# Row tiles of 128 with two meta rows apart, weight blocks visited forward, backward and forward, a written order of the row steps, and a fifth feed-forward unit begun among the first four

## The chip, the cores and the metric

The kernel runs on one core of a Trainium2 chip. Its engines are TensorE (PE), VectorE (DVE), ScalarE (ACT) and GpSimd (POOL); SyncE (SP) issues most of the DMAs. Each engine takes its instructions in the order in which they are queued. The metric is the device time of one execution in microseconds, as the median of several runs.

## The reference, cut to what matters

The program is one decoder layer on 1024 rows of 1024 values. Two mixers (a gated linear recurrence and a pooling mixer) give `z`. The part in question is the product `z @ w_out`, the two norms around the residual, and the start of the gated feed-forward network:

```python
h = h + rmsnorm(z @ w_out[l], mix_norm_post[l])
u = rmsnorm(h, ffn_norm_pre[l])
gt = causal_dwconv(u @ ffn_w_gate[l], ffn_conv_w[l], ffn_conv_b[l])
y = (jax.nn.gelu(gt, approximate=True) * (u @ ffn_w_up[l])) @ ffn_w_down[l]
h = h + rmsnorm(y, ffn_norm_post[l])
return h[:, N_META:]
```

There are 16 meta rows ahead of the 1024. Behind the mixers only the last two are needed, since the convolution looks back over two rows: 1026 rows go through the mixer output and the feed-forward network.

## The kernel before, in words

**Numbers.** Every float32 operand is split into a high and a low part, and a product is three matmuls (`mm3`, L171 to L176): high by high, high by low, low by high. A stationary operand has up to 128 columns, a moving one 512.

**Mixer output.** `z` lies as eight blocks `k` of 128 x 1026, transposed. The output is worked in three chunks `c` of 342 rows, each of three row tiles of 114 (`CW`, `RT`). In a chunk the loop runs over the eight blocks of `w_out`; a block meets the three tiles, two halves of 512 columns and three parts, 18 matmuls. The results `pm` lie in PSUM, a pair of banks a tile, of four pairs. A block of `w_out` is a DMA of 512 KB (`wraw`), a cast to `whi` on ScalarE and, in the first chunk, a low part `wlo` on GpSimd that is also stored to `wlos`. The two later chunks load the raw block and the stored low part again: 24 raw loads and 16 low parts in all. SBUF holds three blocks at a time (`AHEAD`). `split_z` (L1097) makes the high and low part of `z`, one chunk and block at a time.

**Row steps.** A finished tile goes through these steps, which class `Rows` holds: `take` squares it on ScalarE with an accumulator and multiplies it by a gain on DVE; `add` makes the root, the reciprocal and, on DVE, the residual sum, and stores the rows to `hscr`; `norm` squares again and makes `un`; `feat` transposes `un` by eight PE transposes (`pt`) and makes the features in `to_quarters`. The feed-forward product takes the rows as two halves (Strassen's scheme), so the features go to the quarters `b11`, `b21` (first half) and `b12`, `b22` (second half) and to the sums `t1` to `t4`, each with a high part (ScalarE) and a low part (DVE or GpSimd). `by_rows` divides each store and load of a row tile into two DMAs, of 112 and 2 rows.

**Order.** In this part `manual_schedule` is on: PE, ScalarE, DVE and GpSimd run their instructions as the Python code writes them, one list for each engine. SyncE's DMAs are issued as the code reaches them, and wait in one queue. The row steps of a chunk stand between the blocks of the next one; in the last chunk the last three blocks are taken tile by tile.

**The feed-forward units.** `Strassen` plans 22 units of seven products P1 to P7. P1 and P2 need only the first half of the rows, so those of units 0 to 3 (`EARLY`) stand before the rest, with the features of the last three tiles between them; then come P3 to P7 of unit 0 (`rest`) and the other units (`finish`), of which unit 4 (`UP0`) starts with its P1. Weights of these first units are split early and kept in DRAM (`kept`, in the order `KEPT`). `whole` turns finished quarters of a unit into gates, with a convolution on DVE; `swa` and `swb` are sums of weights on GpSimd.

Of the kernel before, what the change touches and what calls it, by code (L numbers as in the profile page):

```python
# [23 lines left out]
CW = TQ // 3  # L24
HEADS = 4
# [34 lines left out]
def trunk_kernel(ctx: ExitStack, tc: tile.TileContext, x, meta_tokens, mix_norm_pre,  # L60
# [117 lines left out]
    def proj(w, col, n_k, xs, chunks, ws=None, name="pj"):  # L178
# [5 lines left out]
        for k in range(n_k):  # L184
            for (lo, n), ps in zip(chunks, banks):
                xhi, xlo = xs(k, lo, n)
                pe.matmul(ps[:, :n], whi[:, k, :], xhi, start=(k == 0), stop=False)
                pe.matmul(ps[:, :n], whi[:, k, :], xlo, start=False, stop=False)  # L188
            for (lo, n), ps in zip(chunks, banks):
                xhi, _ = xs(k, lo, n)  # L190
                pe.matmul(ps[:, :n], wlo[:, k, :], xhi, start=False, stop=(k == n_k - 1))
        return banks

    class Strassen:
# [8 lines left out]
        def __init__(self, units, run, early, quarters, halo, put, whole):  # L203
# [8 lines left out]
            self.got, self.at, self.kept = [], 0, []  # L212
# [118 lines left out]
        def rest(self, u, between=None):  # L331
# [13 lines left out]
            self.whole(u, 0)  # L345
            dve.tensor_tensor(own, own, self.product(u, "P7"), ALU.add)  # L346
            self.put(u, 1, 1, own, x5)
            self.put(u, 1, 0, u2, self.product(u, "P4"))
            self.whole(u, 1)

        def finish(self, at=0):
            for i in range(at, len(self.run)):
                u = self.run[i]
                if i + 1 < len(self.run):
                    self.load_unit(self.run[i + 1])
                if u >= self.early:
                    for f in self.first(u):
                        f()
                self.rest(u)
# [525 lines left out]
    KEPT = [(e + i, p) for e in range(0, EARLY, 2) for p in ("P1", "P2") for i in range(2)]  # L885
    KEPT += [(0, p) for p in Strassen.ORDER[2:]] + [(UP0, p) for p in Strassen.ORDER]
# [211 lines left out]
    def split_z(c, k):  # L1098
        zc = slot(2 * CW, F32R, "zc")
        zh, zl = zc[:, :CW], zc[:, CW:]  # L1100
        act.copy(zh, z[k][:, c * CW : (c + 1) * CW])
        dve.tensor_tensor(zl, z[k][:, c * CW : (c + 1) * CW], rr(zh), ALU.subtract)
# [4 lines left out]
    for kind, i in order:  # L1107
# [23 lines left out]
        banks = proj(None, 0, n_k, xs, chunks, ws=ws, name="p" + kind.lower())  # L1131
# [16 lines left out]
    fq = {}  # L1148
    for n, name, names in ((HT, "v1", ("b11h", "b11l", "b21h", "b21l")), (HN, "v2", ("b22h", "b22l", "t1h", "t1l"))):
        t = ubig(F32R, name).rearrange("p (i k t) -> p i k t", i=4, k=4)  # L1150
# [10 lines left out]
    RT = CW // 3  # L1161
# [4 lines left out]
    def wo_parts(c, k):  # L1166
        if c == 0:
            (hi, lo), = wsplit(wblock(w_out[0], k, 1, 0, D), 1, D, pool_e)
            pool_e.dma_start(wlos[k], rr(lo[:, 0]))
            return [(hi, lo)]  # L1170
# [3 lines left out]
        nc.sync.dma_start(rr(lo), wlos[k])  # L1174
        act.copy(hi, raw)
        return [[t.rearrange("p (k c) -> p k c", k=1) for t in (hi, lo)]]

    wo = Loader([(c, k) for c in range(3) for k in range(KD)], wo_parts)

    def by_rows(move):  # L1180

        for r in (slice(0, RT - HALO), slice(RT - HALO, RT)):
            move(r)

    def load_res(t0):
        row = slot(D, name="row2")
        if t0 == 0:
            nc.sync.dma_start(row[:HALO], meta_tokens[T0:NM, :])
            nc.sync.dma_start(row[HALO:RT], x[0, 0 : RT - HALO, :])
        else:  # L1190
            by_rows(lambda r: nc.sync.dma_start(row[r], x[0, t0 - HALO + r.start : t0 - HALO + r.stop, :]))
# [5 lines left out]
    def to_quarters(un, t_at, banks, eng):  # L1197

        for j in range(2):
            for i in range(4):  # L1200
                k = 4 * j + i
                pe.transpose(banks[j][:, i * RT : (i + 1) * RT], un[:RT, k * P : (k + 1) * P], ident[:RT, :RT])
        srcs = [b_[:, : 4 * RT].rearrange("p (k t) -> p k t", k=4) for b_ in banks]
        n1 = max(0, min(RT, HT - t_at))
        if n1:
            for src, q in zip(srcs, ("b11", "b21")):
                put(q, src[:, :, :n1], slice(t_at, t_at + n1), dve)
        f = max(0, HT - t_at)
        n2 = RT - f
        if n2 <= 0:  # L1210
            return []
        s_ = slice(t_at + f - HT, t_at + RT - HT)
        d = slice(s_.start + HALO, s_.stop + HALO)
        b12, b22 = (src[:, :, f:] for src in srcs)

        t1, t2 = halves_tmp(n2)
        c12, c22 = halves_tmp(n2)
        act.copy(c12, b12)
        act.copy(c22, b22)

        def first_sums():
            combine(dve, t1, c12, ALU.subtract, "b11", d)
            dve.tensor_tensor(t2, c22, t1, ALU.subtract)
            put("t2", t2, d, dve)

        def difference():
            dve.tensor_tensor(c12, c22, c12, ALU.subtract)
            put("t3", c12, s_, dve)

        return [first_sums, lambda: put("t1", t1, s_, dve), lambda: put("b22", c22, s_, eng), difference,  # L1230
                lambda: negdiff(eng, t2, t2, "b21", d), lambda: put("t4", t2, d, eng)]

# [11 lines left out]
    rows, z_at = {}, {}  # L1244

    def next_z(n):

        for i in range(len(z_at), min(len(z_at) + n, 3 * KD)):
            z_at[i] = split_z(i // KD, i % KD)

    def mix_tile(c, k, w, x_, i):
        (whi, wlo), (zh, zl) = w, z_at[c * KD + k]
        t = slice(i * RT, (i + 1) * RT)
        for j in range(2):
            n = slice(j * 512, (j + 1) * 512)
            mm3(x_[:RT, n], (zh[:, t], zl[:, t]), (whi[:, 0, n], wlo[:, 0, n]), k == 0, k == KD - 1)

    class Rows:


        def __init__(self, c, tiles_):
# [422 lines left out]
```

## Time and profile before

| | |
|---|---|
| median of 3 runs | 1365.37 us |
| lowest and highest | 1363.81 and 1366.29 us |
| the profiled execution | 1364.63 us |
| its span in the trace | 1362.9 us |
| mean granted TensorE clock | 0.994 |
| mixer output in the trace | about 595.8 to 707.5 us |

The profile shows one execution. Busy times are of that span; a matmul is pipelined, so its duration overlaps the next, and the distance between two starts is what it costs. A wait names the line of the waiting instruction and, behind the arrow, the engine and line that released it; `DMA` there is a transfer. Names are those of the program's tiles, without numbers.

### The profile page before, as it was taken

Reading aid. Unit: us, or ns where it says so; the run is one execution under the profiler, and the core shown is the slowest. Engines: PE = TensorE matmul, PEld = TensorE weight load, DVE = VectorE, ACT = ScalarE, POOL = GpSimd, SP = SyncE. Lnnn points to the kernel's source line nnn. Section 1 sums busy time; section 2 is a strip of 40 time slices with the busy share of each in tenths; the row PEclk is TensorE's granted clock in tenths of the full one; section 3 lists DMA queues with packets and bytes.
Section 4 is the critical chain, followed back from the end, with each engine's and each line's share of the span. In section 5 each row is a group of like instructions: output and inputs, shape, how many; then the busy total and the mean of one; then the engine's idle time right before and its main releaser. Section 6 shows DMA issues by size and latency. Waiting matters only on the chain. (4 is left out here: it accounts for less than half of the span.)

```text
span 1362.9 us, 20069 instructions
## 1 busy us (share of the span) xinstructions
PE 1338.6 (98%) x7737; PEld 1187.0 (87%) x7737; DVE 955.9 (70%) x1246; ACT 566.2 (42%) x946; POOL 434.1 (32%) x328
## 2 busy tenths in 40 slices
PE   8999999999999999999999999999999999999997
PEld 7799999999999999987779888888888887888786
DVE  6755644489775757766568889888978776744557
ACT  6543333465555474226655222222222223543343
POOL 2014421236343700051020556454557742000100
PEclk9999999998999999999999999999999999999999
DMA  7134333311110159979877877656677799965524
GB/s 266 48 117 140 124 112 106 101 47 47 34 49 19 34 173 306 323 246 301 286 260 245 233 206 201 196 176 164 156 166 170 179 236 269 380 205 191 183 95 154
DMA packets 141453, 236.66 MB, mean 174 GB/s; under 512 B 9254, under 2 KB 77450, under 8 KB 141358
## 3 DMA queue, kind: packets, MB, share of 16 engines
q1 hardware_dynamic: 129294, 211.00, 46.0%
q0 software_dynamic: 12064, 24.38, 10.5%
q8 instruction: 61, 1.00, 0.3%
q14 instruction: 34, 0.28, 0.1%
HBM read 171.85 MB, written 86.53 MB: 190 GB/s over the span
## 5 line engine op out<-in xcount | busy, mean ns | idle before, releaser
L287 PE MATMUL P<-v,whi 128*128 128x512 f32 (+2 forms) x408 | 141.9, 356 | 2.2 <-DVE p L346 1.3
L288 PE MATMUL P<-v,whi 128*128 128x512 f32 (+2 forms) x408 | 141.2, 353 | 0.0
L290 PE MATMUL P<-v,wlo 128*128 128x512 f32 (+2 forms) x424 | 136.0, 351 | 0.0
L175 PE MATMUL pd<-rot 128*128 128x512 f32 x272 | 105.9, 389 | 0.3 <-DVE rot L1417 0.3
L176 PE MATMUL pd<-rot 128*128 128x512 f32 x272 | 105.8, 389 | 0.0
L141 POOL TENSOR_TENSOR wlo<-wraw,whi 128x1024 fp32r<-128x1024 f32 (+1 forms) x19 | 44.7, 2353 | 169.7 <-ACT whi L140 99.1
L1417 DVE TENSOR_TENSOR rot<-yt,rot 128x1024 fp32r<-128x1024 f32 x33 | 41.2, 1249 | 70.1 <-ACT rot L1416 70.1
L287 PEld LDWEIGHTS P<-v,whi 128*128 128x128 f32 x408 | 77.2, 189 | 13.2 <-DVE p L346 1.7
L232 ACT CAST whi<-wraw 128x512 fp32r<-128x512 f32 x78 | 46.1, 618 | 98.1 <-PE P L288 79.1
L288 PEld LDWEIGHTS P<-v,whi 128*128 128x128 f32 x408 | 77.2, 189 | 10.7 <-issue 0.2
L290 PEld LDWEIGHTS P<-v,wlo 128*128 128x128 f32 x424 | 74.3, 189 | 11.4
L233 DVE TENSOR_TENSOR wlo<-wraw,whi 128x512 fp32r<-128x512 f32 x74 | 68.4, 946 | 20.1 <-ACT whi L232 20.1
L1305 POOL TENSOR_TENSOR ys<-y 128x512 f32<-128x512 f32 x22 | 35.6, 1617 | 137.5 <-DVE y L1363 52.6
L174 PE MATMUL pd<-rot 128*128 128x512 f32 x272 | 72.7, 390 | 2.0 <-ACT rot L1416 1.2
L258 POOL TENSOR_TENSOR swa<-wraw,wraw 128x512 f32<-128x512 f32 x28 | 44.4, 1586 | 92.6 <-DMA wraw<-in_w_in_dram 51.2
L140 ACT CAST whi<-wraw 128x1024 fp32r<-128x1024 f32 (+1 forms) x28 | 26.4, 943 | 109.0 <-PE ppv L188 21.7
L1416 ACT CAST rot<-yt 128x1024 fp32r<-128x1024 f32 x33 | 34.6, 1052 | 87.8 <-PE pd L175 87.8
L232 ACT CAST whi<-swa 128x512 fp32r<-128x512 f32 x56 | 33.4, 619 | 85.0 <-PE P L288 76.5
L1349 DVE SCALAR_TENSOR_TENSOR y<-g,par,y 128x1024 f32<-128x1024 f32 x44 | 63.9, 1451 | 0.8
L174 PEld LDWEIGHTS pd<-rot 128*128 128x128 f32 x272 | 50.9, 188 | 13.5 <-ACT rot L1416 1.8
L175 PEld LDWEIGHTS pd<-rot 128*128 128x128 f32 x272 | 51.0, 188 | 11.3 <-DVE rot L1417 0.7
L176 PEld LDWEIGHTS pd<-rot 128*128 128x128 f32 x272 | 51.1, 188 | 10.7
(389 smaller groups left out, 4172.2 us busy)
## 6 DMA issues: line engine op xcount, KB each, us to landing
wraw<-in_w_in_dram SPq DMA_DIRECT2D x36, 512.0 KB
yt<-ysum SPq DMA_DIRECT2D x33, 512.0 KB
wraw<-in_ffn_w_gate_dram SPq DMA_DIRECT2D x26, 512.0 KB
wraw<-in_w_out_dram SPq DMA_DIRECT2D x24, 512.0 KB
wraw<-in_ffn_w_up_dram SPq DMA_DIRECT2D x22, 512.0 KB
wsum<-in_ffn_w_down_dram SPq DMA_DIRECT2D x22, 512.0 KB
ysum<-ys SPq DMA_DIRECT2D x11, 768.0 KB
sa<-sscr SPq DMA_DIRECT2D x16, 513.0 KB
```

The costliest lines, as they stand in the source:

```text
L141: eng.tensor_tensor(lo, raw, rr(hi), ALU.subtract)
L174: pe.matmul(ps, ahi, bhi, start=first, stop=False)
L175: pe.matmul(ps, ahi, blo, start=False, stop=False)
L176: pe.matmul(ps, alo, bhi, start=False, stop=last)
L232: act.copy(hi, src)
L233: (pool_e if 4 <= i < 2 * self.early else dve).tensor_tensor(lo, src, rr(hi), ALU.subtract)
L258: pool_e.tensor_tensor(s1, a21, a22, ALU.add)
L287: pe.matmul(d, whi[:, k, :], xh[:, c : c + w], start=(k == 0 and onto is None), stop=False, **go)
L288: pe.matmul(d, whi[:, k, :], xl[:, c : c + w], start=False, stop=False, **go)
L290: pe.matmul(x[:, o : o + w], wlo[:, k, :], xh[:, c : c + w], start=False, stop=(k == 3), **go)
L1349: dve.scalar_tensor_tensor(a, g[:, j : j + SEQ], cvw[:, j, m : m + 1], a, ALU.mult, ALU.add)
L1417: dve.tensor_tensor(lo, src, rr(hi), ALU.subtract)
```

## The change

**Tiles.** The 1024 rows are eight tiles of 128, in chunks of two, three and three (`TILES`). The two meta rows are a tile of their own in the first chunk (`mix_meta`): high and low part of `z` stand side by side as four stationary columns, so that four matmuls a block do (four columns by `whi` and two by `wlo`, for each half). Low and high results then lie in different rows; `join` copies them out of PSUM, moves two rows by DMA (`pml`), and `joined` adds them.

**Weights.** The blocks are visited 0 to 7, 7 to 0 and 0 to 7 (`KS`). Class `Mixer` keeps the last three blocks over a turn: 18 raw loads and 10 low parts. Every chunk takes its last two blocks tile by tile (`LAST`).

**Row steps.** Class `Row` holds one tile, with `root`, `scale` and `square` as steps of their own. The tables `SEAM` and `SEAM4` write which step stands after which block, tile or product. `negdiff` is always on GpSimd, the low part of `b22` of tiles 4, 5 and 6 too, and that of `t4` for tile 4. Features of the first half are one cast and one subtraction of 1024 columns. Row tiles are stored and loaded by one DMA each.

**Units.** P1 and P2 of unit 4 stand among those of units 2 and 3 (`BEGUN`), and its multiplication by the gate waits for `finish` (`mul_up`). `rest` loads the weights two units ahead, before P4's sums, and unit 0's `whole` of the first half comes after its P7.

**Projection.** The last product before the mixer output (`pba`) does its last two blocks bank by bank (`by_bank`).

```diff
+TILES = ((0, 1), (2, 3, 4), (5, 6, 7))
+KS = (range(8), range(7, -1, -1), range(8))
+LAST = 2
+LATE_ON_POOL = tuple(HALO + i * P for i in (4, 5, 6))
+SEAM = (("W", "W", "W", "W", "W", "W", "0.take 0.add", "W 0.square 1.take m.join 0.norm 1.add 1.square 1.norm"),
+        ("", "W 0.feat 1.load", "W 1.feat m.joined m.take", "W m.add m.square", "W m.norm", "W m.feat", "2.take 2.add", "2.square 3.take 2.norm 3.add", "W 3.square 4.take 3.norm 4.add 4.square 4.norm"),
...
+SEAM4 = ("6.square 5.feat 7.take 6.norm 7.add", "7.square 5.sums 7.norm", "6.feat 5.t2 5.neg 6.sums", "", "7.feat 6.t2 6.neg 7.sums", "7.t2 5.t1 6.t1", "", "7.neg 7.t1 5.b22", "6.b22 5.d3 6.d3 7.b22", "5.t3 7.d3 6.t3 7.t3 5.t4 6.t4 7.t4")
...
-        for k in range(n_k):
+        for k in range(n_k - by_bank):
...
+        for (lo, n), ps in zip(chunks, banks):
+            for k in range(n_k - by_bank, n_k):
+                mm3(ps[:, :n], (whi[:, k, :], wlo[:, k, :]), xs(k, lo, n), False, k == n_k - 1)
         return banks
...
-            self.whole(u, 0)
+            if between is None:
+                self.whole(u, 0)
             dve.tensor_tensor(own, own, self.product(u, "P7"), ALU.add)
+            then("P7")
             self.put(u, 1, 1, own, x5)
-            self.put(u, 1, 0, u2, self.product(u, "P4"))
+            x4 = self.product(u, "P4")
+            if load is not None:
+                self.load_unit(load)
+            self.put(u, 1, 0, u2, x4)
...
-    KEPT = [(e + i, p) for e in range(0, EARLY, 2) for p in ("P1", "P2") for i in range(2)]
-    KEPT += [(0, p) for p in Strassen.ORDER[2:]] + [(UP0, p) for p in Strassen.ORDER]
+    BEGUN = [(e, p) for es in ((0, 1), (2, 3, UP0)) for p in ("P1", "P2") for e in es]
+    KEPT = BEGUN + [(u, p) for u in (0, UP0) for p in Strassen.ORDER[2:]]
...
+        if t_at < HT:
+            src = pt.rearrange("p (j k t) -> p j k t", j=2, k=4) if n == P else pt.rearrange("p j (k t) -> p j k t", k=4)
+            hi, lo = (v1.rearrange("p (j h k t) -> p h j k t", j=2, h=2, k=4)[:, h, :, :, t_at : t_at + n] for h in range(2))
+            act.copy(hi, src)
+            dve.tensor_tensor(lo, src, rr(hi), ALU.subtract)
+            return {}
...
+        neg, t4 = lambda: negdiff(pool_e, t2, t2, "b21", d), lambda: put("t4", t2, d, pool_e if t_at < HT + P else dve)
+        q1, q2 = lambda: put("t1", t1, s_, dve), lambda: put("b22", c22, s_, eng)
...
-            for k in range(KD if c < 2 else KD - 3):
-                w = wo.next()
-                for i in range(3):
-                    mix_tile(c, k, w, tiles_[i], i)
-                if k == KD - 1:
-                    for i in range(3):
-                        own.take(i)
-                wo.ahead()
-                next_z(1)
...
-                        *now, late = last.feat(k - 2) or [None]
-                        for f in now:
-                            f()
...
+            for at in range(KD - LAST):
+                step(c, at)
+                run(*SEAM[c][at].split())
...
+            for n_, i in enumerate(TILES[c]):
+                for j in range(LAST):
+                    mix_tile(c, KD - LAST + j, ws[j], R[i].x, i - TILES[c][0])
+                if n_ + 1 == len(TILES[c]):
+                    if c == 0:
+                        for j in range(LAST):
+                            mix_meta(KD - LAST + j, ws[j], R["m"].x)
+                    if c < 2:
+                        wo.ahead()
+                        begin(c + 1)
...
+        for (e, p), more in zip(BEGUN, SEAM4):
+            (first if p == "P1" else second)(e)
+            run(*more.split())
```

New functions that the code above calls:

```python
    def mix_meta(at, w, x_):
        zm = z_at[at][2]
        for j in range(2):
            n = slice(j * 512, (j + 1) * 512)
            for m, w_ in ((2 * HALO, w[0]), (HALO, w[1]))[:: -1 if at else 1]:
                pe.matmul(x_[:m, n], zm[:, :m], w_[:, n], start=(at == 0 and m > HALO), stop=(at == KD - 1),
                          skip_group_check=True)
...
        def join(self):
            both, self.low = slot(D, name="pmh"), slot(D, name="pml")
            act.copy(both[: 2 * HALO], self.x[: 2 * HALO])
            nc.sync.dma_start(self.low[:HALO], both[HALO : 2 * HALO])
            self.x = both
```

**SyncE's queue around the first turn.** Before, at the end of the first chunk (`hscr` are stored rows, `row` loaded ones, `wlo` a stored low part of weights, `wraw` a raw block):

```order
L1174 DMA wlo_6112<-wlos_5761 128x1024
L1277 DMA hscr<-m_835_6035 112x1024
L1277 DMA hscr<-m_835_6035 2x1024
L1191 DMA row_868_6118<-in_x_dram 112x1024
L1277 DMA hscr<-m_839_6040 112x1024
L1277 DMA hscr<-m_839_6040 2x1024
L1191 DMA row_868_6118<-in_x_dram 2x1024
L1191 DMA row_869_6121<-in_x_dram 112x1024
L1191 DMA row_869_6121<-in_x_dram 2x1024
L1191 DMA row_870_6124<-in_x_dram 112x1024
L1277 DMA hscr<-m_843_6045 112x1024
L1174 DMA wlo_6156<-wlos_5762 128x1024
```

Above, two more of the two-row DMAs stand before the last row shown and are left out as repetitions. Now:

```order
L1348 DMA hscr<-m_830_6003 128x1024
L1322 DMA pml_6048<-pmh_6047 2x1024
L1197 DMA wlo_6089<-wlos_5770 128x1024
L1348 DMA hscr<-m_842_6042 128x1024
L1244 DMA row_864_6132<-in_x_dram 128x1024
L1244 DMA row_865_6134<-in_x_dram 128x1024
L1244 DMA row_866_6136<-in_x_dram 128x1024
L1197 DMA wlo_6115<-wlos_5769 128x1024
```

Twelve row DMAs stood between two reloads of a low part; now four do, and the meta rows' transfer `pml` stands ahead of the first reload.

**ScalarE at the same turn.** Before, the three tiles of the first chunk (`pm_5820` to `pm_5822`) are squared in a row (`junk`), then come the load of a function table, the roots `std` and the second squares `un`:

```order
L1268 ACTIVATE junk_838_6037,ssq_836_6036<-pm_5820 114x1024
L1268 ACTIVATE junk_842_6042,ssq_840_6041<-pm_5821 114x1024
L1268 ACTIVATE junk_846_6047,ssq_844_6046<-pm_5822 114x1024
L1175 CAST whi_6052<-wraw_6050 128x1024
L1101 CAST zc_6056<-sa_5503 128x342
L378 ACT_TABLE_LOAD
L378 ACTIVATE std_6059<-ssq_836_6036,eps_t 114x1
```

Now `pm_5824` is tile 0, `pm_5822` tile 1 and `pm_5823` the meta rows:

```order
L1333 ACTIVATE junk_833_6005,ssq_831_6004<-pm_5824 128x1024
L1337 ACT_TABLE_LOAD
L1337 ACTIVATE std_6008<-ssq_831_6004,eps_t 128x1
L1352 ACTIVATE un_6038,ssq_6037<-m_830_6003 128x1024
L1337 ACTIVATE std_6040<-ssq_6037,eps_t 128x1
L1333 ACTIVATE junk_845_6044,ssq_843_6043<-pm_5822 128x1024
L1321 COPY pmh_6047<-pm_5823 4x1024
```

The square of tile 1, after which its PSUM is free, stands behind the table load and four steps of tile 0.

**GpSimd at the seam to the products.** Before, for two tiles of the middle chunk (one of them in part), the low part of `b22` (`v`), the `negdiff` (two sums `tt`) and the low parts of `t4`, then `swa`. Now, behind the work of tile 4, the sums of tiles 5, 6 and 7:

```order
L1287 TENSOR_TENSOR tt_996_6736<-v_788_5760,tt_996_6736 128x512
L1288 TENSOR_TENSOR tt_996_6736<-v_788_5760,tt_996_6736 128x512
L1287 TENSOR_TENSOR tt_1016_6829<-v_788_5760,tt_1016_6829 128x512
L1288 TENSOR_TENSOR tt_1016_6829<-v_788_5760,tt_1016_6829 128x512
L1287 TENSOR_TENSOR tt_1026_6907<-v_788_5760,tt_1026_6907 128x512
L1288 TENSOR_TENSOR tt_1026_6907<-v_788_5760,tt_1026_6907 128x512
L390 TENSOR_TENSOR v_789_5761<-tt_998_6737,v_789_5761 128x4x128
L390 TENSOR_TENSOR v_789_5761<-tt_1018_6830,v_789_5761 128x4x128
L270 TENSOR_TENSOR swa_7200<-wraw_7196,wraw_7198 128x512
```

All eight stand ahead of the first weight sum `swa`, and none of this work of tiles 5 to 7 was on GpSimd before.

324 lines of the change are left out of this document (170 added, 154 removed), and 2 rows, old and new, of the table SEAM.

## The prediction

> **What bounds the kernel now.** I read the page first, then the PE's waits, then stretches by window, then the PE's timeline around each wait. The page gives each engine's busy time, share and instructions.
>
> ```profile
> PE 1338.6 (98%) x7737; PEld 1187.0 (87%) x7737; DVE 955.9 (70%) x1246; ACT 566.2 (42%) x946; POOL 434.1 (32%) x328
> ```
>
> TensorE sets the time: it is busy 98% of the span, and no other engine passes 70%. So only two things can move the end: the number and pitch of PE instructions, and the few places where PE waits. The next rows are stretches (length, then busy time of PE, PEld, DVE, ACT, POOL, granted clock, DMA share, GB/s): three pieces of the mixer output, the products of the first feed-forward units, and a stretch much later.
>
> ```profile
> 594.47:629.10 34.63, 33.83 (x148) 25.71 (x147) 18.95 (x13) 13.20 (x19) 17.78 (x12) 1.00 0.78 239
> 629.10:670.00 40.90, 39.04 (x182) 29.86 (x181) 22.27 (x32) 26.00 (x47) 0.00 (x0) 1.00 0.85 294
> 670.00:707.53 37.53, 34.70 (x157) 26.32 (x156) 25.58 (x48) 21.11 (x54) 6.43 (x8) 0.95 0.70 244
> 707.53:731.20 23.67, 22.71 (x193) 22.51 (x191) 18.74 (x32) 15.32 (x37) 3.14 (x2) 1.00 0.86 308
> 900.00:1000.00 100.00, 100.00 (x564) 87.56 (x563) 79.49 (x98) 27.52 (x46) 56.28 (x43) 1.00 0.74 188
> ```
>
> From 900 to 1000 us PE never pauses. Work before that which ends earlier therefore ends the program earlier by as much. The mixer has holes in all three pieces, and in the third the granted clock is 0.95. The PE's waits from 594 to 760 us (total, times, longest) name them.
>
> ```profile
> PE pt L1202 <- ACT tt L1219: 2.0, 1, 2.0
> PE pm L175 <- DMA wlo<-wlos: 1.7, 2, 0.9
> PE P L287 <- DVE p L346: 1.3, 1, 1.3
> PE pt L1202 <- DVE v L373: 1.0, 1, 1.0
> PE P L287 <- ACT p L1490: 1.0, 1, 1.0
> PE pm L174 <- DVE sa L853: 0.8, 1, 0.8
> ```
>
> `pt` are the eight transposes of a row tile into features, `wlo` the stored low part of a weight block, `sa` the last sum of the projection before the mixer, `P` the feed-forward products.
>
> **The matmul count.** Before: 3 chunks x 3 tiles x 8 blocks x 2 halves x 3 parts = 432 matmuls `pm`. After: 8 tiles x 8 x 2 x 3 = 384, and 8 x 4 = 32 for the two meta rows: 416. A matmul costs its pitch (the distance between starts), since the durations overlap. Two undisturbed stretches give it with 114 and with 128 stationary columns: the window of `pm` up to the first transposes (198 of them in 45.85 us), and two starts of the timeline, 47 steps of `pv` apart.
>
> ```profile
> 595.75:641.60 45.85, 45.85 (x198) 34.84 (x198) 3.67 (x3) 3.35 (x6) 1.00 0.80 251
> 55.85 0.40 PE L174 MATMUL pv<-whi,uhi 128*128 128x512 f32 x1
> 66.52 0.39 PE L176 MATMUL pv<-wihi,ulo 128*128 128x512 f32 x1
> ```
>
> 45.85/198 = 0.2315 us, 10.67/47 = 0.227. No row has a stationary of 4 or 2 columns in a long stretch; it gets the longer pitch. So 432 x 0.2315 = 100.0 becomes 384 x 0.227 + 32 x 0.2315 = 94.6: 5.4 saved, and I take 5.2, because the 114-wide rows may owe part of their longer pitch to their place and not to their width. Bounds: all 416 at the old pitch save 3.7, all at 0.227 save 5.6. The transposes stay 9 x 8.
>
> The Trainium skill, page "TensorE: Matmul & The Clock Gate", section "Back-to-back issue gap", makes the isolated gap N/2.4 + 2.5 ns, 216 ns at N = 512, whatever the stationary columns. By it only the 16 missing matmuls would count, an estimate of 3.5 us; the rows above lie 5 to 7% over that gap and differ with the width, so I go by the rows.
>
> **The waits that go.** The PE's timeline (start, duration, line, instruction, idle before it) around each wait:
>
> ```profile
> 594.31 0.63 PE L191 MATMUL pba<-ah,wlo 128*128 128x342 f32 x3
> 595.75 0.46 PE L174 MATMUL pm<-whi,zc 128*114 128x512 f32 x1 [0.80 <-DVE sa L853]
> ...
> 647.25 0.47 PE L174 MATMUL pm<-whi,zc 128*114 128x512 f32 x1
> 648.59 0.49 PE L175 MATMUL pm<-wlo,zc 128*114 128x512 f32 x1 [0.87 <-DMA wlo<-wlos]
> ...
> 652.38 0.39 PE L176 MATMUL pm<-whi,zc 128*114 128x512 f32 x1
> 653.76 0.97 PE L1202 MATMUL pt<-ident,un 114*128 114x114 f32 x8 [0.99 <-DVE v L373]
> ...
> 690.23 0.39 PE L176 MATMUL pm<-whi,zc 128*114 128x512 f32 x1
> 692.67 1.00 PE L1202 MATMUL pt<-ident,un 114*128 114x114 f32 x8 [2.05 <-ACT tt L1219]
> 693.76 0.63 PE L175 MATMUL pm<-wlo,zc 128*114 128x512 f32 x1
> ...
> 696.75 0.56 PE L176 MATMUL pm<-whi,zc 128*114 128x512 f32 x1
> ...
> 731.22 0.39 PE L287 MATMUL P<-v,whi 128*128 128x258 f32 x1 [0.98 <-ACT p L1490]
> ...
> 752.42 0.50 PE L287 MATMUL P<-v,whi 128*128 128x512 f32 x1 [1.27 <-DVE p L346]
> ```
>
> What a wait costs is the late start: the start found, less the previous start plus one pitch; that is the idle time shown and about 0.15 to 0.2 more, since a duration overlaps the next start.
>
> *Start of the mixer:* the last three `pba` would end their pitch at 594.31 + 3 x 0.16 = 594.8, and `pm` starts at 595.75: 1.0. The projection's last two blocks now finish bank by bank, so its first two sums are complete 12 and 6 matmuls before the end, 1.9 and 1.0 us at that pitch, and the first tile takes banks that are free by then. Taken: 1.0; bounds 0 and 1.0.
>
> *Late low parts:* 1.1 (648.59 against 647.25 + 0.31, and a restart 0.1 slower), and 1.0 for the second of that group. The transfer came late because of its place in SyncE's queue:
>
> ```profile
> 642.87 0.34 SPq L1174 DMA_DIRECT2D wlo<-wlos  x1
> ```
>
> It was issued at 642.87 and waited for at 648.59, 5.7 us. Ahead of it stood the stores and loads of the last chunk's rows, two DMAs each. Now a row tile is one DMA, and the first reload after a turn is of the fourth block used, because three are still held: 3 blocks x 18 matmuls x 0.227 = 12.3 us after the turn. The added meta transfer `pml<-pmh` stands ahead of it in this queue and waits for ScalarE's copy; 12.3 against 5.7 covers that. In the last chunk block 7 has about 6 us, the thin place. Taken: both go, 2.1; bound: both stay.
>
> *Late transposes:* 653.76 - 652.61 = 1.15, and 692.67 - 690.46 = 2.2. Each waited for the sums and copies of the tile before on DVE and ScalarE, written as one block; the new order gives them one or more blocks of 4.1 us each. After the second, eight matmuls start 0.427 apart (693.76 to 696.75, seven steps) and not 0.2315: 8 x 0.196 = 1.6, the 0.95 of the window. Taken: 4.95; the low bound leaves one of the short waits, 1.15, in place.
>
> *First units:* idle 0.98 and 1.27, and with the 0.15 to 0.2 late by 1.2 and 1.5. Both wait for DVE or ScalarE to finish what the last tiles and products left. The fifth unit's P1 and P2, 24 matmuls x 0.23 = 5.5 us of PE, now stand ahead. They are work that was due later anyway, so PE loses nothing. Taken: 2.7; bounds 0 and 2.7.
>
> Sum of gains: 5.2 + 1.0 + 2.1 + 4.95 + 2.7 = 15.95.
>
> **The waits that come.** No row shows them, so each is bounded by its nearest ones.
>
> ```profile
> L1268 ACT ACTIVATE junk<-pm 114x1024 f32<-114x1024 f32 x9 | 9.2, 1023 | 1.1 <-PE pm L176 1.1
> 631.75 1.28 ACT L378 ACT_TABLE_LOAD   x1
> L1276 DVE SCALAR_TENSOR_TENSOR m<-m,rstd,row 114x1024 f32<-114x1024 f32 x9 | 11.7, 1299 | 0.3
> ```
>
> *First turn:* tile 4 reuses the PSUM of tile 1. Tile 1's `take` is written behind tile 0's `add` and `square`. From the end of tile 0 ScalarE and DVE hand on in turn: square with its accumulator 1.2, table load 1.3, root 0.3, DVE's reciprocal and add 1.5, the second square 1.2, its root 0.3, tile 1's square 1.2: 7.0, and some 0.15 at each of seven hand-overs, 8.0. PE has tile 1's 12 matmuls, the meta rows' 8 and tiles 2 and 3 for cover: 2.7 + 1.9 + 2.7 = 7.3. With the slower restart, taken: -1.0, between 0 and -1.5 (one more row instruction). Behind the late take stand the meta copy and tile 1's norm, which have blocks to spare.
>
> *Meta features:* two rows pay as much for each step as 128. Seven dependent steps of 1.0 to 1.3 us, with the other row steps between, come to some 13 us, and PE reaches the transposes 12.3 us after the last feature set. Taken: -0.7; bounds 0 and -1.5.
>
> *Sums on GpSimd:* in the seam to the products GpSimd gets three tiles' `negdiff` (two operations) and two `b22` low parts. What that does to DVE shows once before:
>
> ```profile
> 698.55 0.63 DVE L1223 TENSOR_TENSOR tt<-tt,tt 128x456 f32<-128x456 f32 x1
> 700.95 1.53 DVE L1227 TENSOR_TENSOR tt<-tt 128x456 f32<-128x456 f32 x1
> 701.96 1.48 POOL L1241 TENSOR_TENSOR tt<-v,tt 128x456 f32<-128x456 f32 x1
> ```
>
> The same DVE shape took 0.63 alone and 1.53 beside GpSimd. At 1.48 for 456 columns an operation is 1.7 for 512, so eight are 11 to 13 us; the others (1.1) are shorter, and I take 11. In them DVE loses 0.90 of every 1.53: 6.5 us. Its cover is its idle time in the 707.53 row, 23.67 - 18.74 = 4.9, and the 5.5 us of the begun unit: 10.4. Taken: -0.3; bounds 0 and -3. If the cover were gone, the 6.5 would be paid.
>
> The Trainium skill, page "SBUF — State Buffer", section "Who interferes with whom", says that a DVE instruction with two SBUF inputs and a GpSimd instruction that reads SBUF exclude each other and the later one fully blocks. The slowed operation agrees in direction, with 0.90 us lost against GpSimd operations of 1.1 to 1.5. With full blocking DVE could lose all 11 us, an estimate, 0.6 over the cover: 1351.7 in place of 1351.4.
>
> The remaining edits cost nothing: fewer loads (18 raw blocks and 10 low parts for 24 and 16) lie beside PE in a mixer at a DMA share of 0.70 to 0.85, and the reordered loads and sums of later units lie under the PE that is busy without a pause at 900 to 1000. Without that cover a 512 KB load such as the `wlo` above would show its 5.7 us.
>
> **Sum.** 15.95 - 2.0 = 13.95. The profiled execution took 1364.63 (its span 1362.9 and 1.7 around it), so it becomes 1350.7; it lies 0.74 under the median of 1365.37, so the median becomes 1351.4. All bounds at their best: 5.6 + 1.0 + 2.1 + 4.95 + 2.7 = 16.4, 1349.0. All at their worst: 3.7 + 3.8 for the transposes - 1.5 - 1.5 - 3.0 = 1.5, 1363.9.
>
> **Rivals.**
>
> *No new wait* (0.10): the seven-step chains fit. For it: the margins at the turn and the meta features are below 1 us. Time 1349.
>
> *GpSimd holds up the seam* (0.20): DVE's 6.5 us meet a `t4` or `t3` product before the cover helps, because the begun unit runs before those sums and its own copies queue behind them. For it: the 1.53 row; against: 10.4 us of cover. It gives 4 to 6.5 back: 1355.4 to 1358.
>
> *Only the count* (0.09): the 10.75 us of waits return under other names, since ScalarE and DVE do the same sums: 1365.4 - 5.2 = 1360.2. Against it: 594 to 707 us has DVE busy 67 of 113.
>
> *Slower through the clock* (0.06): transposes now come when their norm is late, each with a wait like that at 692.67: 2.2, and the slow stretch, 1.6: 3.8 a time. There are nine; the gain of 14 and the 2.7 that can be told from no change are used up from the fifth on. With six, 1351.4 + 22.8 = 1374. Against it: one of nine did this before, and waits of 1.15 and 1.45 left the pitch whole.
>
> The Trainium skill, page "TensorE: Matmul & The Clock Gate", section "What's actually happening", halves the clock after an idle window of some 3.4 us and restores it after as long a busy one. The slow stretch, 3.4 us, agrees with the second; the idle before it was 2.05, so the first is not what this trace shows. By that rule a wait of 2.2 would cost no slow stretch, and six would make 1351.4 + 13.2 = 1364.6.
>
> *Not what it says:* the order could leave a tile's matmuls or loads where they were. The written order shows 416 `pm` and the reloads ahead of the row DMAs, so I give this no chance of its own.
>
> **Chances.** The forecast 0.55, the rivals 0.10, 0.20, 0.09 and 0.06. Runs of this kernel can tell 0.2%, 2.7 us, from no change. All but the last two cases are faster; of the 0.09 I count 0.04 as within 2.7: faster 0.90, same 0.04, slower 0.06. The range takes the forecast, no new wait and the GpSimd case: 1348 to 1358; 1 below 1349 for what the fewer transfers may free.
>
> **What would show it.** Right: `pm` 416 at 0.227 to 0.23; no wait on `wlo`; no stretch of pitch 0.43 and a clock of 1.00 in the mixer; `pm` waiting once for a PSUM release near 1 us; the third product of unit 0 and unit 4 without a wait. Wrong: a wait of `P` on a DVE low part with GpSimd rows beside it; `pt` waits over 2 us; a pitch of 0.2315 with 128 columns.

## The result and the profile after

| | before | after |
|---|---|---|
| median | 1364.59 us | 1350.24 us |
| lowest and highest | 1362.81 and 1366.29 us | 1349.08 and 1353.47 us |
| ratio, 95% interval | | 0.9899, 0.9876 to 0.9922 |
| profiled execution, span | 1362.9 us | 1349.6 us |

The kernel is faster, by 10.6 to 16.9 us of 1365 by the interval. The page after, in its line of busy times, and the PE's waits from 580 to 760 us:

```profile
PE 1330.9 (99%) x7721; PEld 1184.0 (88%) x7721; DVE 975.9 (72%) x1232; ACT 561.8 (42%) x931; POOL 440.4 (33%) x331
```

```profile
PE pm L183 <- ACT junk L1333: 0.8, 1, 0.8
```

Of seven waits in that stretch one is left. It is a new one: the first turn, which waits for ScalarE's square of tile 1. The next rows measure two stages from start to start, the mixer output (first `pm` to first `P`) and the seam (first `P` to the end of unit 4), before and then after. Columns: length, busy time of PE, PEld, DVE, ACT, POOL, granted clock, DMA share, GB/s.

```profile
595.75:707.53 111.78, 107.08 (x481) 81.66 (x481) 65.72 (x89) 59.27 (x118) 24.11 (x20) 0.98 0.78 262
707.53:769.14 61.61, 59.36 (x385) 53.65 (x384) 51.23 (x79) 27.61 (x62) 14.47 (x11) 1.00 0.76 256
```

```profile
595.13:696.24 101.11, 100.33 (x466) 79.33 (x465) 62.69 (x78) 52.92 (x99) 22.28 (x15) 1.00 0.69 235
696.24:755.50 59.26, 59.25 (x385) 53.93 (x384) 53.60 (x70) 29.79 (x62) 23.88 (x19) 1.00 0.76 248
```

The mixer is 10.67 us shorter and the seam 2.35. PE is busy 59.25 of 59.26 us in the seam, where it lacked 2.25 before. The start of the mixer and the first turn are in the PE's timeline after:

```profile
594.98 0.32 PE L185 MATMUL pba<-ah,wlo 128*128 128x342 f32 x1
595.13 0.40 PE L183 MATMUL pm<-whi,zc 128*128 128x512 f32 x1
...
626.98 0.39 PE L185 MATMUL pm<-whi,zc 128*128 128x512 f32 x1
628.14 0.50 PE L183 MATMUL pm<-whi,zc 128*128 128x512 f32 x1 [0.78 <-ACT junk L1333]
...
633.76 1.04 PE L1255 MATMUL pt<-ident,un 128*128 128x128 f32 x8
634.56 0.49 PE L183 MATMUL pm<-whi,zc 128*128 128x512 f32 x1
```

The first `pm` follows the last `pba` by one pitch, 0.15. Before, it came 1.44 us after the first of three `pba` and 0.47 of that was theirs: 0.97 saved. So the three places give 10.67 + 0.97 + 2.35 = 13.99. The span is shorter by only 13.3. The projection before the mixer would have ended at 594.78 and ended at 595.13 in this execution, 0.35 later; and unit 4 ended 13.64 earlier, but the last matmul of the chain (1355.70 before, 1342.54 now) 13.16. No row here tells where the 0.48 behind unit 4 went.

ScalarE's timeline at the first turn shows what the one wait is made of:

```profile
625.61 1.06 ACT L1352 ACTIVATE un<-m 128x1024 f32<-128x1024 f32 x1 [1.55 <-DVE m L1347]
626.58 0.18 ACT L1352 ACTIVATION_READ_ACCUMULATOR un<-m 128x1 f32 x1
626.79 0.30 ACT L1337 ACTIVATE std<-ssq,eps_t 128x1 f32<-128x1 f32 x1
627.00 1.00 ACT L1333 ACTIVATE junk<-pm 128x1024 f32<-128x1024 f32 x1
```

Tile 1's `junk` starts at 627.00, behind tile 0's `un` and `std`, and PE goes on at 628.14.

### The profile page after: what moved, and what is told of

Its sections match the earlier page's. It is cut to its first block, busy times and chain, and to the rows that moved or that the text cites. A ratio compares the mean times of both kernels' runs of the same rounds, so it can differ in the third digit from the quotient of the medians.

```text
span 1349.6 us, 19941 instructions
## 1 busy us (share of the span) xinstructions
PE 1330.9 (99%) x7721; PEld 1184.0 (88%) x7721; DVE 975.9 (72%) x1232; ACT 561.8 (42%) x931; POOL 440.4 (33%) x331
## 5 line engine op out<-in xcount | busy, mean ns | idle before, releaser
L300 PEld LDWEIGHTS P<-v,whi 128*128 128x128 f32 x408 | 77.2, 189 | 10.5
L270 POOL TENSOR_TENSOR swa<-wraw,wraw 128x512 f32<-128x512 f32 x28 | 40.9, 1462 | 134.2 <-DMA wraw<-in_ffn_w_gate_dram 70.4
L245 DVE TENSOR_TENSOR wlo<-swb,whi 128x512 fp32r<-128x512 f32 x56 | 62.7, 1126 | 6.7 <-ACT whi L244 6.6
L245 DVE TENSOR_TENSOR wlo<-wraw,whi 128x512 fp32r<-128x512 f32 x74 | 62.4, 865 | 1.4 <-ACT whi L244 1.4
L244 ACT CAST whi<-swb 128x512 fp32r<-128x512 f32 x56 | 33.4, 618 | 68.4 <-PE P L300 64.7
L185 PEld LDWEIGHTS pd<-rot 128*128 128x128 f32 x272 | 51.0, 188 | 10.6
L300 PE MATMUL P<-t4l,whi 128*128 128x258 f32 (+1 forms) x196 | 57.1, 308 | 0.0
```

Of the source, the lines that this page charges most:

```text
L185: pe.matmul(ps, alo, bhi, start=False, stop=last)
L244: act.copy(hi, src)
L245: (pool_e if 4 <= i < 2 * self.early else dve).tensor_tensor(lo, src, rr(hi), ALU.subtract)
L270: pool_e.tensor_tensor(s1, a21, a22, ALU.add)
L300: pe.matmul(d, whi[:, k, :], xl[:, c : c + w], start=False, stop=False, **go)
```

## The experiments

Each kernel is timed against the kernel before on the same chip, and the ratio is to that; 1 to 4, 5 to 8 and 9 to 12 ran on three different chips, so medians of different groups compare less well than ratios. Lengths of the mixer and the seam are taken from one trace each, from start to start as above, and tell differences of a few tenths, where the runs of one kernel scatter by 2 to 11 us.

| kernel | median us | ratio, 95% interval | mixer | seam |
|---|---|---|---|---|
| before | | | 111.78 | 61.61 |
| after | 1350.24 | 0.9899, 0.9876 to 0.9922 | 101.11 | 59.26 |
| 1 projection not bank by bank | 1350.52 | 0.9900, 0.9870 to 0.9931 | 101.08 | 59.00 |
| 2 all forward | 1356.15 | 0.9936, 0.9913 to 0.9958 | 107.22 | 59.00 |
| 3 rows in 126 and 2 | 1352.70 | 0.9911, 0.9884 to 0.9938 | 102.99 | 59.23 |
| 4 early take | 1348.71 | 0.9882, 0.9855 to 0.9908 | 99.87 | 59.23 |
| 5 unit 4 not begun | 1356.13 | 0.9936, 0.9914 to 0.9959 | 100.97 | 64.67 |
| 6 sums on DVE | 1350.31 | 0.9896, 0.9865 to 0.9928 | 101.01 | 59.00 |
| 7 forward, rows in 126 and 2 | 1364.42 | 0.9997, 0.9978 to 1.0016 | 116.11 | 59.00 |
| 8 before, 128 columns | 1365.11 | 1.0006, 0.9989 to 1.0024 | 111.64 | 61.28 |
| 9 before, 512-byte steps | 1364.12 | 0.9991, 0.9975 to 1.0006 | 110.74 | 62.49 |
| 10 after, shifted by 56 bytes | 1350.07 | 0.9878, 0.9843 to 0.9912 | 102.62 | 59.00 |
| 11 rows in 112 and 16 | 1352.73 | 0.9900, 0.9870 to 0.9930 | 102.18 | 59.24 |
| 12 forward, rows in 112 and 16 | 1361.53 | 0.9965, 0.9950 to 0.9980 | 111.38 | 59.24 |

### 1. The projection not bank by bank

```diff
-                     by_bank=2 if (kind, i) == ("BA", KD - 1) else 0)
+                     by_bank=0)
```

> The changed kernel with the last projection block finished for all its sums together, as before. Theory (banks come free early): the first pm waits again for DVE's last sum sa, 0.8 us idle, and the mixer starts 1.0 us late; everything after it keeps its length (101.1 us from the first pm to the first P); span +1.0, about 1350.6. Rival (the new tiles lie in other PSUM banks, so that alone takes the wait away): no wait, span unchanged within 0.3.

The wait is back, 0.80 on DVE's `sa`, and the first `pm` comes 1.44 us after the last group of `pba`, as before. The mixer keeps its length (101.08). The place of the new tiles in PSUM alone does not remove the wait. In the median the 1 us does not show: its four runs reach from 1348.33 to 1355.28.

### 2, 3 and 7. The order of the blocks and the row DMAs

```diff
-KS = (range(8), range(7, -1, -1), range(8))
+KS = (range(8), range(8), range(8))
```

```diff
-            nc.sync.dma_start(row, x[0, t0 - HALO : t0 - HALO + P, :])
+            for r in (slice(0, P - HALO), slice(P - HALO, P)): nc.sync.dma_start(row[r], x[0, t0 - HALO + r.start : t0 - HALO + r.stop, :])
```

The second edit splits the stores in the same way. The first kernel has the first edit, the second the second, the third both.

> The changed kernel with the weight blocks visited 0 to 7 in all three chunks, so 24 raw loads and 16 low parts; nothing else changed. Theory (the turn gives the reloads their time): at the two turns the second block is asked for only when the chunk's last matmuls release a buffer, 5.7 us before it lands; ScalarE's cast waits for it with the row steps queued behind, PE waits 3 to 6 us at each turn; together +6 to +12 us. Rival (reloads were never the point, transfers hide anyway): within 1 us of the changed kernel.

> The changed kernel with each store and load of a row tile in two DMAs (126 and 2 rows) as before the change. Theory (the reload after a turn has some 12 us of lead): no wait on wlo, no change within 0.5 us. Rival (the single DMAs took the wlo waits away): pm waits for wlo again at a turn, about 1 us each, +2.

> The changed kernel with the blocks 0 to 7 in all chunks and each row tile's DMAs in two. Theory: the forward visits cost as in that run alone, the doubled row DMAs stand ahead of the reloads and add up to 2 us more. Rival (the queue hardly matters): the same time as all forward alone, within 0.5.

Forward alone costs 6.1 us of mixer, at the low end of what was expected, but not in the way expected. The PE's timeline of that kernel at the second turn:

```profile
663.90 0.63 PE L183 MATMUL pm<-whi,zc 128*128 128x512 f32 x1 [2.65 <-ACT whi L1201]
664.33 0.63 PE L184 MATMUL pm<-wlo,zc 128*128 128x512 f32 x1
```

PE waits for the cast `whi` of the first block, not for its transfer. ScalarE was not held by a late load: the cast stands behind the row steps of the turn and starts at 662.82. With the turn this cast does not exist, because the block is still held. The wait is followed by eight matmuls 0.427 apart, about 1.6 us more. At the first turn three shorter waits (0.74, 0.41 and 0.33) stand in place of the one of 0.78.

Rows in two brought back what the theory had excluded. Of the changed kernel with rows in two, a window of five us and the PE's wait:

```profile
638.40:643.40 5.00, 5.00 (x23) 4.13 (x23) 3.76 (x4) 2.59 (x5) 0.00 (x0) 1.00 1.03 246
```

```profile
648.26 0.50 PE L184 MATMUL pm<-wlo,zc 128*128 128x512 f32 x1 [1.72 <-DMA wlo<-wlos]
```

And the changed kernel itself after its row loads:

```profile
635.00:640.00 5.00, 5.00 (x28) 4.19 (x27) 1.69 (x2) 2.35 (x4) 0.00 (x0) 1.00 1.01 388
```

The DMA engines are as busy (1.03 and 1.01), but move 246 GB/s in place of 388. The reload that waits left SyncE's queue at 637.70, which is half a microsecond later than in the changed kernel (638.75) when the 1.58 us by which this mixer started earlier are added. Most of its delay is thus not in the queue: its last piece landed at 648.22, 10.5 us after it was issued, and in the changed kernel at 645.06, after 6.3. That the pieces of rows issued ahead of it kept the engines is the likely reason.

Both edits together cost 15.0, not 6.1 + 1.9, and far more than the 2 on top that the expectation allowed: the whole gain of the change is gone, the ratio is 0.9997. The likely reason is that the forward order needs more transfers (24 raw blocks and 16 low parts for 18 and 10) just where the split rows slow them. Its longest PE waits in the mixer:

```profile
PE pm L183 <- ACT whi L1201: 4.7, 3, 2.6
PE pm L184 <- DMA wlo<-wlos: 4.3, 3, 2.0
```

### 4. Tile 1 taken early

```diff
-SEAM = (("W", "W", "W", "W", "W", "W", "0.take 0.add", "W 0.square 1.take m.join 0.norm 1.add 1.square 1.norm"),
+SEAM = (("W", "W", "W", "W", "W", "W", "0.take 0.rootm", "W 1.take 0.add 0.square m.join 0.norm 1.add 1.square 1.norm"),
```

Here `rootm` is the root that `add` makes otherwise.

> The changed kernel with tile 1's take written behind tile 0's root and ahead of tile 0's add and square: DVE multiplies tile 1 in its idle time and ScalarE squares it before tile 0's second square. Theory (tile 4 waits for tile 1's PSUM, which ScalarE's order holds): the 0.8 us wait of pm on junk goes, the mixer takes 100.1 us in place of 101.1, span -1.0. Rival (something else gates tile 4, such as the meta copy or the table load): the wait stays, or moves to another releaser, 0.

ScalarE at the turn of this kernel:

```profile
622.70 0.30 ACT L1337 ACTIVATE std<-ssq,eps_t 128x1 f32<-128x1 f32 x1
622.99 1.03 ACT L1333 ACTIVATE junk<-pm 128x1024 f32<-128x1024 f32 x1
```

`junk` of tile 1 now starts right after tile 0's root, and PE has no wait in the mixer: 99.87, 1.24 less. Its median, 1348.71, is the lowest of all, but its interval overlaps with that of the change, and the kernel of experiment 10, with a mixer 2.75 us longer, has as low a ratio: the gain is read from the trace, not from the whole runs.

### 5. Unit 4 not begun early

```diff
-    BEGUN = [(e, p) for es in ((0, 1), (2, 3, UP0)) for p in ("P1", "P2") for e in es]
-    KEPT = BEGUN + [(u, p) for u in (0, UP0) for p in Strassen.ORDER[2:]]
+    BEGUN = [(e, p) for es in ((0, 1), (2, 3)) for p in ("P1", "P2") for e in es]
+    KEPT = BEGUN + [(0, p) for p in Strassen.ORDER[2:]] + [(UP0, p) for p in Strassen.ORDER]
```

The steps of the two entries of `SEAM4` that fall away go to the entry before.

> The changed kernel with unit 4's P1 and P2 back behind unit 0, so the row steps and sums of tiles 5 to 7 stand among eight products and not ten. Theory (5.5 us of unit 4 are the cover of DVE's late sums): P waits for t3 or t4 low parts, 3 to 5 us in all, +4. Rival (the new order of steps alone keeps the seam clear): no wait of P over 0.5 us, 0.

The seam is 5.4 us longer. The DVE's last sum and PE's wait for it:

```profile
737.15 0.76 DVE L390 TENSOR_TENSOR t4l<-tt,t4h 128x256 fp32r<-128x256 f32 x2 [0.19 <-ACT t4h L389]
```

```profile
738.61 0.36 PE L299 MATMUL P<-t4h,whi 128*128 128x258 f32 x1 [2.89 <-issue]
```

Three waits (0.49 on a `v`, 1.38 on `t3l`, 2.89 here) and their restarts make the 5.4. The last row is put down to "issue", but it follows by 0.1 the end of the sum that DVE makes right behind `t4l`, and the changed kernel does the same. First that sum in the kernel without unit 4, then both in the changed kernel:

```profile
737.83 0.69 DVE L350 TENSOR_TENSOR p<-p,P 128x514 f32<-128x514 f32 x1
```

```profile
737.33 0.76 DVE L390 TENSOR_TENSOR t4l<-tt,t4h 128x256 fp32r<-128x256 f32 x2 [0.19 <-ACT t4h L389]
738.01 0.68 DVE L350 TENSOR_TENSOR p<-p,P 128x514 f32<-128x514 f32 x1
```

```profile
738.40 0.39 PE L302 MATMUL P<-t3h,wlo 128*128 128x512 f32 x1
738.79 0.36 PE L299 MATMUL P<-t4h,whi 128*128 128x258 f32 x1
```

`p` is the sum that reads P6 of unit 0 out of PSUM. The product with `t4`, P4, stands four products behind P6, and there are four pairs of banks, so P4 needs the pair that this sum frees. It ends at 738.52 and 738.69, and P4 starts 0.1 later each time. What PE waits for is thus not the low part itself, which ended at 737.91 and 738.09, but the sum that stands in DVE's queue behind all of the late sums. Counted from the first `P`, it ends within 0.3 us at the same moment with and without unit 4's products, and in the changed kernel PE, whose P4 starts 0.39 after its predecessor and not 0.23, arrives 0.16 us too early: the cover is used up.

### 6. All sums on DVE

```diff
-LATE_ON_POOL = tuple(HALO + i * P for i in (4, 5, 6))
+LATE_ON_POOL = ()
...
-        neg, t4 = lambda: negdiff(pool_e, t2, t2, "b21", d), lambda: put("t4", t2, d, pool_e if t_at < HT + P else dve)
+        neg, t4 = lambda: negdiff(dve, t2, t2, "b21", d), lambda: put("t4", t2, d, dve)
```

> The changed kernel with all negdiff, b22 and t4 low parts of the second half on DVE and none on GpSimd. Theory (GpSimd's sums cost DVE about what they take from it): DVE gets some 6 us of operations and loses the 6 us by which it was slowed; its two-input operations take 0.7 for 512 columns throughout; P does not wait more than 0.5 us, span within 0.5. Rival A (GpSimd's sums are a real relief): P waits 1 us or more for t3l or t4l, +1 to +5. Rival B (they are a burden on the path): -0.5 or more.

The theory holds. In this kernel DVE makes a sum of 512 columns in 0.69 until the weight sums start:

```profile
709.99 0.69 DVE L1288 TENSOR_TENSOR tt<-v,tt 128x512 f32<-128x512 f32 x1
...
712.04 0.69 DVE L1272 TENSOR_TENSOR tt<-tt,tt 128x512 f32<-128x512 f32 x1
```

In the changed kernel the same place on DVE and GpSimd:

```profile
710.06 1.47 DVE L1282 TENSOR_TENSOR tt<-tt,v 128x512 f32<-128x512 f32 x1
711.56 1.47 DVE L1272 TENSOR_TENSOR tt<-tt,tt 128x512 f32<-128x512 f32 x1
```

```profile
709.56 1.42 POOL L1287 TENSOR_TENSOR tt<-v,tt 128x512 f32<-128x512 f32 x1 [8.33 <-PE P L300]
711.06 1.43 POOL L1288 TENSOR_TENSOR tt<-v,tt 128x512 f32<-128x512 f32 x1
```

Each of these sums on GpSimd costs DVE 0.78, and on DVE it would have cost 0.69. The rows show how: the two engines take turns. DVE's sum of 710.06 ends at 711.53, 0.55 after GpSimd's first sum ended (710.98), and the one of 711.56 ends 0.55 after GpSimd's second (712.49). That second sum, begun at 711.06, ends 0.96 after DVE's had ended. So whichever starts later does its work when the other is done, and its duration contains that wait. Later in the same trace all 19 DVE sums `wlo<-wraw,whi` of L245 that start within a GpSimd sum end 0.54 to 0.56 after it, while 19 sums `p<-p,P` of L359, which take one input from PSUM, keep their 0.68 to 0.69.

The seam is 59.00 in place of 59.26, but that is not the sums' doing: kernels 1, 2, 7 and 10 leave them on GpSimd and have 59.00 too. In all five PE meets no wait at P4.

### 8, 9 and 10. Width and place of the stationary operand

The first widens two of three tiles of the kernel before, the second lays its three pieces of `zc` 128 columns apart, the third shifts the high parts of the changed kernel by 56 bytes and the low parts by 112:

```diff
+        w_ = RT if i == 2 else P
-        t = slice(i * RT, (i + 1) * RT)
+        t = slice(i * RT, i * RT + w_)
...
```

```diff
-        zc = slot(2 * CW, F32R, "zc")
-        zh, zl = zc[:, :CW], zc[:, CW:]
+        zc = slot(6 * P, F32R, "zc")
+        zh, zl = (zc[:, h * 3 * P : (h + 1) * 3 * P].rearrange("p (i t) -> p i t", t=P)[:, :, : CW // 3] for h in range(2))
...
```

```diff
-        zh, zl = zc[:, :n], zc[:, n : 2 * n]
+        zh, zl = zc[:, 14 : 14 + n], zc[:, 28 + n : 28 + 2 * n]
...
```

> The kernel before with 128 stationary columns instead of 114 for the first two of the three tiles of each chunk (14 columns of the next tile are computed once more and not used). Theory (width sets the pitch): 288 of the 432 matmuls take 0.227 in place of 0.2315, the mixer is 1.2 us shorter, span -1.2. Rival (the place in the program sets it): the pitch of all stays 0.2315, no change.

> The kernel before with the three 114-column pieces of zc laid 128 columns apart, so each stationary operand starts at a multiple of 512 bytes and not at multiples of 456 (low parts at 1368). The width stays 114. Theory (where the stationary operand lies sets the pitch): pitch of pm from 0.231 to 0.227, mixer from 111.8 to about 110.1 us. Rival (neither place nor width; the matmuls' surroundings): 0.231 and 111.8.

> The changed kernel with the high and low parts in zc starting 56 and 112 bytes later, so no stationary operand of 128 columns starts at a multiple of 512 bytes. Theory (place sets the pitch): 0.2278 becomes 0.230 or more, the mixer 102 us or more in place of 101.1. Rival: 0.228 and 101.1.

The mean distance of successive `pm` starts, from the PE's timeline without the places at transposes and waits:

| columns | place | pitch us |
|---|---|---|
| 114 | steps of 456 bytes (before) | 0.2311 |
| 128, and 114 for a third | steps of 456 bytes (8) | 0.2300 |
| 114 | steps of 512 bytes (9) | 0.2301 |
| 128 | steps of 512 bytes, shifted by 56 and 112 (10) | 0.2320 |
| 128 | steps of 512 bytes (after) | 0.2280 |

Neither width nor place alone gives the short pitch; the kernel with both has it. Even the 0.0011 of the eighth kernel are not the width's: its widened matmuls take 0.2304 and the ones left at 114 columns 0.2293. The one clean pair is the last: 384 x 0.0040 = 1.5, and the mixer of the shifted kernel is 102.62, 1.5 longer. That width matters once the place is right (0.2301 against 0.2280) rests on two different kernels and is not shown alone. In the ninth kernel only 0.4 of the 1.0 us comes from the pitch (432 x 0.0010). The rest is a wait like that at 692.67 before, which here has no slow stretch behind it (1.6), less longer waits elsewhere:

```profile
692.81 1.00 PE L1203 MATMUL pt<-ident,un 114*128 114x114 f32 x8 [2.04 <-ACT tt L1220]
693.57 0.47 PE L174 MATMUL pm<-whi,zc 128*114 128x512 f32 x1
693.88 0.39 PE L175 MATMUL pm<-wlo,zc 128*114 128x512 f32 x1
```

The seam of that kernel is 0.9 longer than before, which no expectation covers, so its whole time is unchanged.

### 11 and 12. Rows in 112 and 16

```diff
-            nc.sync.dma_start(row, x[0, t0 - HALO : t0 - HALO + P, :])
+            for r in (slice(0, 112), slice(112, P)): nc.sync.dma_start(row[r], x[0, t0 - HALO + r.start : t0 - HALO + r.stop, :])
```

The stores are split alike; the second of these kernels also visits the blocks forward.

> The changed kernel with each row tile's store and load in two DMAs of 112 and 16 rows, against the 126 and 2 of the earlier run, which had a wlo wait of 1.7 us while the DMA engines were busy throughout at 250 GB/s. Theory (126 rows make the transfer itself slow): no wlo wait, mixer 101.1 within 0.3. Rival (the number of DMAs in the queue ahead of the reload): the wait of 1 to 2 us is back, mixer 102.5 or more.

> All forward, with row DMAs of 112 and 16 rows. Theory (126 rows slow the transfers): as all forward with whole rows, mixer 107.2, within 1. Rival (two DMAs for one in the queue): as forward with 126 and 2, mixer about 116.

The theory falls for the most part, and the rival's 102.5 is not reached either. With 112 and 16 rows the wait on `wlo` is back at 0.91, the mixer is 1.07 longer, and the engines again move 257 GB/s at a full share:

```profile
638.40:643.40 5.00, 5.00 (x28) 4.23 (x27) 1.98 (x2) 1.01 (x1) 0.00 (x0) 1.00 1.03 257
```

All forward with this split takes 111.38, between 107.22 with whole rows and 116.11 with 126 and 2, so both expectations missed. So two pieces for one cost transfer time, and 126 and 2 cost more than 112 and 16. Why a split row keeps the engines longer is not settled; the runs only show it.

## Why the prediction was right

*The sum.* Predicted 13.95 us. The three places measured 13.99 in the trace, the medians 14.35. The predicted time of 1351.4 lies 1.2 above the median.

*The matmul count, 5.2.* Right in size. 432 `pm` at the measured 0.2311 are 99.8, 416 at 0.2280 are 94.8: 5.0. Its reason was only half right. Sixteen matmuls fewer are 3.7, which the text had as its lower bound. The other 1.3 is not the width alone: widening gave 0.0011 of a pitch difference of 0.0031, and not in the widened matmuls. The short pitch was seen only with 128 columns that also start at steps of 512 bytes.

*The start of the mixer, 1.0.* Measured 0.97, and the run without the bank-by-bank end brings back its 0.80 of idle time.

*Late low parts, 2.1.* The waits went, as said. The step that failed is the lead, "12.3 us after the turn" against 5.7: this is the first reload, and the third is the tight one. Every reload is issued when a buffer comes free, two blocks and a set of transposes ahead of its use: the third at 638.75 at the earliest, for matmuls at 648 to 650 us. The rows as single DMAs were not a side matter; undone they cost 1.1 to 1.9 with the turn, 4.2 to 8.9 more without it.

*Late transposes, 4.95.* No wait of `pt` and no stretch at 0.43 is left in the mixer. The reason given, sums and copies "written as one block", does not go far enough back. Before, ScalarE stood idle ahead of both late sets:

```profile
649.85 1.05 ACT L1175 CAST whi<-wraw 128x1024 fp32r<-128x1024 f32 x1 [4.84 <-DMA wraw<-in_w_out_dram]
687.71 1.05 ACT L1175 CAST whi<-wraw 128x1024 fp32r<-128x1024 f32 x1 [4.87 <-DMA wraw<-in_w_out_dram]
```

Each cast waited for a late raw block, and the copies of the set of transposes before it, a set that PE had done by 647.5 and 685.4, stood behind the cast in ScalarE's queue. So these waits too go back to late loads. In the changed kernel no idle time before a cast of the mixer is put down to a load. No run puts the old order of the feature steps back alone, so what the written order adds is not shown. And 1.6 of this term, the slow stretch, is not certain in the kernel before either: the ninth kernel had the same wait, 2.04, without it; the eighth, with 2.06, had it.

*First turn, -1.0.* Right to the tenth: 628.14 - 627.21 = 0.93 and a restart 0.1 slower. The order named as its cause was the cause, since taking tile 1 early removes it.

*Meta features, -0.7.* No wait: the norm of the two rows was ready. *Transposes, 0.* Mis-sized: the text left them at "9 x 8", but a set of a wide tile takes PE 0.79 (633.76 to 634.56) and 0.71 before (713.29 to 714.00); with 0.58 for the meta rows' set the nine take about 0.5 more. That the two errors nearly cancel is luck.

*Sums on GpSimd, -0.3.* The price was near: beside the six sums and two low parts on GpSimd, DVE loses 0.4 to 1.1 in each of eight operations, 6.4 in all against 6.5. The cover was too large: "10.4" was compared with 6.5, and 3.9 should have been left, but -0.16 was. Missing in the sum were the weight sums `swa` and `swb`, which stand next on GpSimd: beside them a `t3l` and three `t4l` take some 1.51 each on DVE, where one takes 0.42 alone, 4.4 more. 6.4 and 4.4 are 10.8, the cover and a little. The rival "GpSimd holds up the seam" was thus nearer than its 0.20 said; what kept it away is unit 4, whose 5.5 us of products the seam needs in full.

*First units, 2.7.* The two waits are gone; 2.35 was measured, and 0.24 of the difference are three sets of wider transposes. Taken alone the term was undersized: without unit 4 the new order would be 5.4 slower than it is, and the seam 3.1 longer than before.

The Trainium skill's rule that the later instruction fully blocks ("SBUF — State Buffer", "Who interferes with whom") is what the rows of experiment 6 show. The prediction's "all 11 us" by it was too much, because it took GpSimd's durations as work: the 1.43 of a sum contains 0.47 of waiting for DVE, and alone it needs 0.96.

The rival of six slow stretches did not come: no transposes wait. The Trainium skill's rule of a 3.4 us idle window ("TensorE: Matmul & The Clock Gate", "What's actually happening") is not what these runs show: waits of 2.65 and of 2.04 to 2.06 were followed by a slow stretch, others of 2.04, 2.05 and 2.89 were not. A window that runs freely, which that page of the Trainium skill also states, would fit that the same wait goes both ways, but not a slow stretch after 2.05 if all of a window has to be idle; no run here tests it.

## What to carry to other kernels

Where PE is busy to 98%, count matmuls and late starts: a sum of late starts from the timeline came within 3% of the gain, while shares of busy time said nothing of it. Edits that look independent (a turn in the order of weights, one DMA per tile) can cover for each other, so each must be undone both alone and together with the other before it is called free. A wait is put down to the instruction that released it, but what held that one can be another engine's queue: the late transposes and P4 were both found one step further back. Where an order is written by hand, look at the first instruction that frees a buffer and put it ahead of the work that nobody waits for.

## What the runs showed of the hardware that was not expected

Moving the stationary operands of 128 columns by 56 bytes (high parts) and 112 (low parts) lengthened the pitch of 512-column matmuls from 0.2280 to 0.2320 us.

A row tile moved as two DMAs and not one left the DMA engines as busy, at 1.03, while they moved 246 to 257 GB/s in place of 388.

An idle time of 2.04 to 2.06 us was followed by some eight matmuls at 0.427 in three kernels (before, 7 and 8) and by none in two (9 and 12).

DVE sums with both inputs in SBUF and GpSimd sums took turns: a DVE sum of 512 columns that began within a GpSimd sum ended 0.55 us after it. It lost 0.78 to a GpSimd sum, and takes 0.69 alone, so moving one there neither helped nor hurt.
